# Forgetting attention in a two-layer trunk: negated scores, mask in the bias row, query blocks from last to first, normalisation moved from the probabilities to the output

## The chip, the cores and the metric

One core of a Trainium2 chip runs the whole kernel. The metric is the device time of one execution in microseconds (us); lower is better. A core has TensorE (PE in the profile, with its weight loads as PEld), VectorE (DVE), ScalarE (ACT), GpSimd (POOL), SyncE (SP, which issues the DMAs here), a working memory SBUF of 128 partitions and an accumulation memory PSUM of eight banks.

## The reference, cut to what matters

The trunk has two layers: attention and an MLP, then a state-space mixer and an MLP, each between RMS norms. Batch 1, 1024 positions, 1024 channels, 16 heads of 64. Only the attention is touched:

```python
proj = h @ w_in                     # q, k, v, gate (1024 columns each), f_logit (16)
q = rmsnorm(heads(q), q_gain)
k = rmsnorm(heads(k), k_gain)
log_f = log_sigmoid(f_logit + b_f)
c = cumsum(log_f, axis=1).transpose(0, 2, 1)
scale = HEAD_DIM ** -0.5
for blk in range(seq_len // Q_BLOCK):              # 8 blocks of 128 queries
    ...
    s = einsum('bhqd,bhkd->bhqk', qb, kb) * scale  # keys up to the block's end
    s = s + c[:, :, q0:k_end, None] - c[:, :, None, :k_end]
    s = where(mask, s, -inf)                       # causal
    p = softmax(s, axis=-1)
    outs.append(einsum('bhqk,bhkd->bhqd', p, vb))
o = concatenate(outs) ...
o = o * sigmoid(gate)
return o @ w_out
```

The term c of the query is the same along a row, so softmax drops it: the kernel adds only the key's term.

## The kernel before, in words

The kernel is written with a tile framework: the program names tiles, and the order of each engine's queue and all its waits are fixed when the kernel is built, from the order of writing, from priorities (`high_priority`), and from estimated durations. On the chip each engine then works its queue strictly in order. `weave` alternates between streams of work in the order of writing: each stream is a generator that yields a cost after each piece, and the stream that is least far through its total goes next.

The attention handles one pair of heads at a time (`fox`, line 613). Beside the attention of pair hp run the projections of pair hp+1 (`qkv`, 466) and the gate of pair hp-1 (`gate`, 506); beside the last pair only the gate before and the output weights. Products of fp32 data are made of parts rounded to fp32r: projections by `fm` (277) and `mm3` (271, lines 273 to 275) with three matmuls for high and low halves.

`forget_sum` (388) makes the running sum of the forget terms, with the sign turned so that it is minus c, and stores it to DRAM as `negc`. `attend` (525) goes through 128 units, 16 heads by 8 query blocks, block 0 first; block qb has (qb+1)x128 keys. For a unit:

- `load_bias` (531) brings the head's row of `negc` to all 128 partitions, as tile `An` (two buffers, SyncE's queue).
- `scores` (535) multiplies queries and keys into a PSUM slot of two banks (lines 543, 544; two such slots). VectorE adds the causal mask to the diagonal block (546), adds the bias row and takes the row maximum in one instruction (548, with a small accumulator read), and turns its sign (550). ScalarE takes the exponential with that as bias and accumulates the row sum (553). VectorE takes the reciprocal (554), and GpSimd multiplies the whole row block by it (555).
- `transposes` (557), one unit later, turns the probabilities by blocks of 128 on TensorE (567), four blocks to a PSUM bank. There is one bank for this (`PTB`). ScalarE copies the high part out (570, tile `pth`), VectorE the rest (571, `ptl`). These have three buffers each.
- `values` (573), after every second unit, multiplies with v (586) into one PSUM bank; after two such, ScalarE and VectorE add the halves into `o` (590, 591).

`qk_proj`, `qk_norm` and `v_proj` (400 to 464) leave their PSUM banks through ScalarE and VectorE (409 and 457 among them); line 437 copies the queries to the other half of the partitions on GpSimd. `gate` multiplies `o` by the sigmoid (518) and stores the result; the last pair's stays on the chip (`ogk`) and is split for the output product (254, 255). Weights come on SyncE's queue (232).

Of the kernel before, what the change touches and what calls it, by code (L numbers as in the profile page):

```python
# [11 lines left out]
AF = mybir.ActivationFunctionType  # L12
ALU = mybir.AluOpType

P = 128
D = 1024
NT = 8
NH = 16
HD = 64
FF = 2816  # L20
NF = FF // P
EPS = 1e-6
NEG = -1e30
NPG = 38
LNEXP = 'natural_log_exp_and_others'
MAGIC = 1.5 * 2.0 ** 23
# [6 lines left out]
PTB = (2,)  # L33
# [3 lines left out]
def f32(ap):  # L37
    return ap.bitcast(F32)
# [121 lines left out]
class Trunk:  # L160
# [178 lines left out]
    def fox_setup(self):  # L339
        nc, A, c = self.nc, self.A, self.cst  # L340
        self.bones = c.tile([P, P], F32R, name="bones")
        nc.vector.memset(f32(self.bones), 0.0)
        for i in range(2):
            nc.vector.memset(f32(self.bones[i * 64:i * 64 + 64, i * 64:i * 64 + 64]), 1.0)
        self.cmask = c.tile([P, P], F32, name="cmask")
        nc.gpsimd.memset(self.cmask, 0.0)
        nc.gpsimd.affine_select(out=self.cmask, in_=self.cmask, compare_op=ALU.is_ge, fill=NEG, base=0,
                                pattern=[[-1, P]], channel_multiplier=1)
        self.gcol = []
        for nm_, s in (("fox_q_gain", HD ** -0.5), ("fox_k_gain", 1.0)):  # L350
            t = c.tile([P, 1], F32, name=nm_ + "c")
            v = A[nm_]
            for i in range(2):
                nc.sync.dma_start(t[i * 64:i * 64 + 64, :],
                                  bass.AP(tensor=v.tensor, offset=v.offset, ap=[[1, HD], [1, 1]]))
            nc.vector.tensor_scalar_mul(t, t, -0.5 * s)
            self.gcol.append(t)
        self.bf = c.tile([NH, 1], F32, name="bf")
        v = A["fox_b_f"]
        nc.sync.dma_start(self.bf, bass.AP(tensor=v.tensor, offset=v.offset, ap=[[1, NH], [1, 1]]))  # L360
        self.wf = self.R("wf", (P, 8, 48), F32R)
        raw = self.R("wr", (P, 8, NH))
        nc.sync.dma_start(raw, A["fox_w_in"][0][:, 4 * D:4 * D + NH].rearrange("(k p) n -> p k n", p=P))
        nc.gpsimd.memset(f32(self.wf[:, :, NH:32]), 0.0)
        nc.gpsimd.tensor_copy(self.wf[:, :, 0:NH], raw)
        nc.gpsimd.tensor_sub(self.wf[:, :, 32:48], raw, f32(self.wf[:, :, 0:NH]))
        self.negc = self.dram("negc", [NH, D])

    def forget_logits(self, hT):
        nc, R = self.nc, self.R  # L370
# [17 lines left out]
    def forget_sum(self):  # L388

        nc = self.nc  # L390
        z, t1, ones = self.fgt
        nc.scalar.activation(t1, z, AF.Abs)
        nc.scalar.activation(t1, t1, AF.Exp, scale=-1.0)
        nc.scalar.activation(t1, t1, AF.Ln, bias=self.one[0:NH])
        nc.vector.tensor_scalar_mul(z, z, -1.0)
        nc.vector.scalar_tensor_tensor(t1, z, 0.0, t1, op0=ALU.max, op1=ALU.add)
        nc.vector.tensor_tensor_scan(z, ones, t1, 0.0, op0=ALU.mult, op1=ALU.add)
        nc.sync.dma_start(self.negc, z)

    def qk_proj(self, w, hT, hf, st):  # L400
        nc = self.nc
# [122 lines left out]

    def attend(self, c, o):

        nc = self.nc
        units = [(h, qb) for h in range(NH) for qb in range(8)]
        An, pt, Pt, pv = {}, {}, {}, {}

        def load_bias(h):
            An[h] = self.R("An")
            nc.sync.dma_start(An[h], self.bcast(self.negc[h:h + 1, :], D))

        def scores(h, qb):
            qh, ql = c[h // 2]["q"][h % 2 * 2:h % 2 * 2 + 2]
            k = c[h // 2]["k"][h % 2]
            nk = (qb + 1) * P
            qs = slice(qb * P, nk)
            ps = self.S("S")  # L540
            for c0 in range(0, nk, 512):
                c1 = min(c0 + 512, nk)
                nc.tensor.matmul(ps[:, c0:c1], qh[:, qs], k[:, c0:c1], start=True, stop=False)
                nc.tensor.matmul(ps[:, c0:c1], ql[:, qs], k[:, c0:c1], start=False, stop=True)
            with self.tc.high_priority(AHEAD):
                nc.vector.tensor_add(ps[:, qs], ps[:, qs], self.cmask)
                m, nm = self.small("mx"), self.small("nm")
                nc.vector.tensor_tensor_reduce(out=ps[:, :nk], in0=ps[:, :nk], in1=An[h][:, :nk], op0=ALU.add, op1=ALU.max,
                                               scale=1.0, scalar=-3e38, accum_out=m)
                nc.vector.tensor_scalar_mul(nm, m, -1.0)  # L550
            p = Pt[h, qb] = self.R("Pt")
            rs, ri = self.small("rs"), self.small("ri")
            nc.scalar.activation(p[:, :nk], ps[:, :nk], AF.Exp, bias=nm, accum_out=rs)
            nc.vector.reciprocal(ri, rs)  # L554
            nc.gpsimd.tensor_scalar(p[:, :nk], p[:, :nk], ri, 1.0, op0=ALU.mult, op1=ALU.mult)  # L555

        def transposes(h, qb):
            j, qq = qb // 2, qb % 2
            if qq == 0:
                ng = (2 * j + 2 + 3) // 4  # L560
                pt[h, j] = [(self.R("pth", (P, 4, 256), F32R), self.R("ptl", (P, 4, 256), F32R)) for _ in range(ng)]
            p = Pt.pop((h, qb))
            for g in range(0, qb + 1, 4):
                n = min(4, qb + 1 - g)
                p2 = self.pb(PTB, (P, 4, P))
                for i in range(n):
                    nc.tensor.transpose(p2[:, i], p[:, (g + i) * P:(g + i + 1) * P], self.ident)  # L567
                th, tl = pt[h, j][g // 4]
                dh, dl = th[:, 0:n, qq * P:qq * P + P], tl[:, 0:n, qq * P:qq * P + P]
                nc.scalar.copy(dh, p2[:, 0:n])  # L570
                nc.vector.tensor_sub(dl, p2[:, 0:n], f32(dh))  # L571

        def values(h, j):
            h2, vt = h % 2, c[h // 2]["v"]
            if h2 == 0 and j == 0:
                o[h // 2] = self.R("o")
            r = slice(h2 * 64, h2 * 64 + 64)
            if j % 2 == 0:
                pv[h] = self.pb(PVB)
            out = pv[h][:, (j % 2) * 256:(j % 2) * 256 + 256]  # L580
            last = 2 * j + 1
            t = pt.pop((h, j))
            seq = [(0, 0)] + [(kb, i) for kb in range(1, last + 1) for i in (0, 1)] + [(0, 1)]
            for n, (kb, i) in enumerate(seq):
                lo = P if kb == last else 0
                nc.tensor.matmul(out[:, lo:], vt[kb // 4][:, kb % 4, h2, :], t[kb // 4][i][:, kb % 4, lo:],
                                 start=(n == 0), stop=(n == len(seq) - 1))
            if j % 2:
                d = o[h // 2][r, (j // 2) * 512:(j // 2) * 512 + 512]
                nc.scalar.copy(d, pv[h][64 - h2 * 64:128 - h2 * 64])  # L590
                nc.vector.tensor_add(d, d, pv[h][r])

        load_bias(0)
        for i in range(len(units) + 3):
            hp = min(i, len(units) - 1) // 16
            if i < len(units):
                h, qb = units[i]
                if qb == 0:
                    yield 0.0, hp
                scores(h, qb)  # L600
                if qb == 5 and h + 1 < NH:
                    load_bias(h + 1)
                yield 0.16 * (qb + 1), hp
            if 1 <= i <= len(units):
                h, qb = units[i - 1]
                transposes(h, qb)
                yield 0.11 * (qb + 1), hp
            if i >= 3 and (i - 3) % 2 == 1:
                h, qb = units[i - 3]
                values(h, qb // 2)  # L610
                yield 0.22 * (qb + 1), hp
# [837 lines left out]
def trunk(ctx: ExitStack, tc: tile.TileContext, A, out):  # L1449
    T = Trunk(ctx, tc, A, out)  # L1450
    nc, R = T.nc, T.R
    rg = lambda a, b: list(range(a, b))
# [35 lines left out]
    for f in range(8):  # L1488
        T.plan(T.cols(A["s5_w_glu"][0], f * P)[:3] + (("glu",) * 2 if f == 0 else (None,) * 2))
        if f >= 1:  # L1490
# [11 lines left out]
          cc=[33], cp=[34, 13, 17], T=[33, 7, 14], M=[30, 16, 18], rot=[29, 10, 15], u=[25, 8, 9], Z=[4], k=[6],  # L1502
          S5=[26, 11, 3], Y=[27], W=[28, 32], gt=[31, 32], sg5=[33], gtk=[34])

    R.set(**{f"p{i}": [i] for i in [*range(7, 15), 35]}, vt=rg(15, 19), pth=rg(19, 22), ptl=rg(22, 25), pt=rg(25, 29) + [23, 24], An=[29, 30], Pt=[31, 32],
          o=[33, 34], x=[15, 16, 17, 18, 22, 13], y=[30, 12, 14], gn=[33], wf=[34], wr=[32], fg=[19, 20, 21])
    x0 = A["x"][0]
    hT = T.new_hT()
# [121 lines left out]
```

## Time and profile before

| | before |
|---|---|
| time, median of 3 runs | 2474.95 us (2472.84 to 2478.91) |
| the profiled execution's own time | 2474.52 us |
| its span in the profile | 2472.7 us |
| attention's period, one pair of heads | 79 us |
| mean granted TensorE clock | 0.99 |

The profile is of one execution. A row of groups reads: line, engine, operation, output and inputs with shapes, count, busy us and mean ns of one, idle time of the engine before them and what ended it. In a view of waits, "PEld ps L567 <- DVE ptl L571: 2.0, 5, 0.6" says that weight loads of line 567 waited 2.0 us in all, 5 times, at most 0.6 us, for VectorE's line 571. A matmul's end is modelled in the profile, so a busy TensorE is not one at its peak. In a timeline the columns are start, duration (us), engine, line, operation, and in brackets the idle time before with what ended it.

### The profile page before, as it was taken

What the parts mean: (1) busy time and instruction counts of PE and PEld (TensorE: products, weight loads), DVE (VectorE), ACT (ScalarE), POOL (GpSimd) and SP (SyncE); (2) the same over time, 40 slices, a digit from 0 to 9 for tenths busy, and PEclk for the clock granted to TensorE, in tenths of its full rate; (3) what the DMA queues carried; (4) which work ended last, traced back from release to release, by engine and by line L of the source; (5) the groups of instructions that cost most, each with busy time, mean ns of one, the idle gap of its engine ahead of it and who ended that gap; (6) DMA issues with size and microseconds to landing.
All of it is one profiled execution on the core that took longest, in us unless ns stands there. A gap on an engine that the chain in (4) does not pass through costs nothing.

```text
span 2472.7 us, 31528 instructions
## 1 busy us (share of the span) xinstructions
PE 2370.7 (96%) x11484; PEld 1938.5 (78%) x11484; DVE 1758.2 (71%) x3050; ACT 1177.2 (48%) x1989; POOL 554.0 (22%) x452
## 2 busy tenths in 40 slices
PE   7999999999998999999989989899999999999998
PEld 5777778777777778888877768788878888888886
DVE  6877877778778957666588785774686556555867
ACT  5766676667745343444434543332463333333434
POOL 3323222223200034545571241430000000000003
PEclk9999999999999999999999999999999999999999
DMA  4121111111243434343678742544334233337874
GB/s 128 54 60 43 43 44 52 44 43 56 87 148 97 122 116 130 118 133 113 225 248 273 268 158 74 153 144 127 108 100 130 90 115 103 98 111 248 287 237 160
DMA packets 251083, 314.50 MB, mean 127 GB/s; under 512 B 33888, under 2 KB 179488, under 8 KB 250928
## 3 DMA queue, kind: packets, MB, share of 16 engines
q1 hardware_dynamic: 250928, 312.50, 39.5%
q8 instruction: 90, 1.47, 0.2%
q14 instruction: 65, 0.53, 0.1%
HBM read 234.79 MB, written 77.66 MB: 126 GB/s over the span
## 4 chain that ended last, share of the span: by engine, by line
PE 53%; DVE 6%; DMA 2%; ACT 2%; issue 2%; POOL 1%; SPq 0%; DVEq 0%; ACTq 0%; POOLq 0%
PE ps L790 30%; PE ps L886 11%; PE ps L273 3%; PE ps L275 3%; PE ps L274 3%; DMA raw<-in_ffn_w_down_dram 1%; DVE wdl L255 1%; DMA raw<-in_s_w_in_dram 1%; DVE gl L255 1%; PE ps L1274 0%; POOL S L1256 0%; PE ps L1273 0%; PE ps L1232 0%; DVE y L315 0%; DMA gr<-g_d 0%
## 5 line engine op out<-in xcount | busy, mean ns | idle before, releaser
L790 PE MATMUL ps<-B,ah 128*128 128x512 f32 x1056 | 330.0, 394 | 4.0 <-ACT cc L1107 2.3
L886 PE MATMUL ps<-wdl,gh 128*128 128x512 f32 x616 | 243.8, 396 | 14.5 <-DVE wdl L255 13.7
L886 PE MATMUL ps<-wdh,gh 128*128 128x512 f32 x616 | 243.2, 395 | 6.5 <-DVE m L906 3.7
L886 PE MATMUL ps<-wdh,gl 128*128 128x512 f32 x616 | 242.7, 394 | 1.8 <-DVE gl L255 1.8
L790 PEld LDWEIGHTS ps<-B,ah 128*128 128x128 f32 x1056 | 200.7, 190 | 47.8 <-ACT cc L1107 2.7
L790 PE MATMUL ps<-ops,ah 128*128 128x512 f32 x704 | 218.1, 391 | 1.9 <-ACT s L830 1.9
L273 PE MATMUL ps<-hT,wh 128*128 128x512 f32 x512 | 207.8, 406 | 9.0 <-DVE pt L409 4.3
L555 POOL TENSOR_SCALAR Pt<-Pt,ri 128x128 f32<-128x128 f32 (+7 forms) x128 | 117.8, 921 | 415.5 <-DVE ri L554 327.0
L790 PE MATMUL ps<-B,al 128*128 128x512 f32 x528 | 207.4, 393 | 0.0
L274 PE MATMUL ps<-hT,wh 128*128 128x512 f32 x512 | 203.7, 398 | 0.0
L275 PE MATMUL ps<-hT,wl 128*128 128x512 f32 x512 | 203.0, 397 | 0.0
L1581 POOL TENSOR_TENSOR y<-m,s 128x512 f32<-128x512 f32 x4 | 7.2, 1794 | 765.7 <-DMA raw<-in_ffn_w_down_dram 756.8
L254 ACT CAST gh<-gr 128x1024 fp32r<-128x1024 f32 (+1 forms) x78 | 81.2, 1041 | 202.3 <-PE ps L886 138.3
L255 DVE TENSOR_TENSOR gl<-gr,gh 128x1024 fp32r<-128x1024 f32 (+1 forms) x78 | 110.3, 1416 | 82.1 <-ACT gh L254 79.0
L761 DVE TENSOR_TENSOR al<-raw,ah 128x1024 fp32r<-128x1024 f32 x88 | 112.9, 1283 | 64.1 <-ACT ah L760 64.0
L790 PEld LDWEIGHTS ps<-ops,ah 128*128 128x128 f32 x704 | 131.4, 188 | 30.9 <-ACT s L830 2.4
L886 PEld LDWEIGHTS ps<-wdl,gh 128*128 128x128 f32 x616 | 117.4, 191 | 42.9 <-DVE wdl L255 18.5
L760 ACT CAST ah<-raw 128x1024 fp32r<-128x1024 f32 x88 | 92.6, 1052 | 112.0 <-PE ps L790 107.2
L571 DVE TENSOR_TENSOR ptl<-ps,pth 128x512 fp32r<-128x512 f32 (+1 forms) x192 | 106.3, 554 | 55.2 <-ACT pth L570 50.0
L886 PEld LDWEIGHTS ps<-wdh,gh 128*128 128x128 f32 x616 | 117.6, 191 | 33.7 <-DVE m L906 4.1
L886 PEld LDWEIGHTS ps<-wdh,gl 128*128 128x128 f32 x616 | 117.5, 191 | 26.6 <-DVE gl L255 2.3
L570 ACT CAST pth<-ps 128x512 fp32r<-128x512 f32 (+1 forms) x192 | 91.8, 478 | 95.8 <-PE ps L567 83.7
(342 smaller groups left out, 5962.2 us busy)
## 6 DMA issues: line engine op xcount, KB each, us to landing
raw<-in_ffn_w_down_dram SPq DMA_DIRECT2D x98, 512.0 KB, 5.0
gr<-g_d SPq DMA_DIRECT2D x76, 512.0 KB, 4.5
raw<-in_ffn_w_gate_dram SPq DMA_DIRECT2D x44, 512.0 KB, 4.1
raw<-in_ffn_w_up_dram SPq DMA_DIRECT2D x44, 512.0 KB, 4.3
g_d<-s SPq DMA_DIRECT2D x66, 256.0 KB, 2.1
raw<-in_fox_w_in_dram SPq DMA_DIRECT2D x32, 512.0 KB, 4.1
g_d<-up SPq DMA_DIRECT2D x22, 512.0 KB, 2.7
g_d<-up SPq DMA_DIRECT2D x44, 256.0 KB, 2.7
```

Source lines behind the costliest of these rows:

```text
L254: self.nc.scalar.copy(h, src)
L255: self.lsub.tensor_sub(l, src, f32(h))
L273: mm(ps, lh, rh, start=start, stop=False)
L274: mm(ps, lh, rl, start=False, stop=False)
L275: mm(ps, ll, rh, start=False, stop=stop)
L555: nc.gpsimd.tensor_scalar(p[:, :nk], p[:, :nk], ri, 1.0, op0=ALU.mult, op1=ALU.mult)
L570: nc.scalar.copy(dh, p2[:, 0:n])
L571: nc.vector.tensor_sub(dl, p2[:, 0:n], f32(dh))
L760: nc.scalar.copy(h, src)
L761: V.tensor_sub(l, src, f32(h))
L790: nc.tensor.matmul(bank, x[:, k], y, start=start and k == i == 0, stop=True, skip_group_check=True)
L886: nc.tensor.matmul(bank, x[:, j, t], y[:, j], start=start and i == 0, stop=True, skip_group_check=True)
```

## The change

Scores are made negative: the query gain gets a minus sign, the stored sum is c itself, and what was a maximum becomes a minimum, which the exponential takes as its bias directly with scale -1. The mask is positive (1e30) and is added by GpSimd to the head's bias row, at the diagonal block's columns, ahead of each unit; since the blocks of a head now go from last to first, a masked block of the row is needed by no later unit. The probabilities stay undivided. The row sums of a pair's 16 units are gathered in one tile, transposed, inverted, stored to DRAM and read back as two broadcasts (64 partitions for each head), and GpSimd multiplies the pair's output `o` with them ahead of the gate. The order of `transposes` and `values` follows the reversed blocks, and the second group of transposes of a unit is written after one more yield. The tile of broadcast reciprocals has two buffers.

```diff
-NEG = -1e30
+FAR = 1e30
...
-        nc.gpsimd.affine_select(out=self.cmask, in_=self.cmask, compare_op=ALU.is_ge, fill=NEG, base=0,
+        nc.gpsimd.affine_select(out=self.cmask, in_=self.cmask, compare_op=ALU.is_ge, fill=FAR, base=0,
...
-        for nm_, s in (("fox_q_gain", HD ** -0.5), ("fox_k_gain", 1.0)):
+        for nm_, s in (("fox_q_gain", -HD ** -0.5), ("fox_k_gain", 1.0)):
...
-        self.negc = self.dram("negc", [NH, D])
+        self.csum = self.dram("csum", [NH, D])
+        self.ri_d = [self.dram(f"ri{hp}_d", [NH, P]) for hp in range(8)]
...
-        nc.vector.tensor_scalar_mul(z, z, -1.0)
-        nc.vector.scalar_tensor_tensor(t1, z, 0.0, t1, op0=ALU.max, op1=ALU.add)
+        nc.vector.scalar_tensor_tensor(t1, z, 0.0, t1, op0=ALU.min, op1=ALU.subtract)
         nc.vector.tensor_tensor_scan(z, ones, t1, 0.0, op0=ALU.mult, op1=ALU.add)
-        nc.sync.dma_start(self.negc, z)
+        nc.sync.dma_start(self.csum, z)
...
-        units = [(h, qb) for h in range(NH) for qb in range(8)]
-        An, pt, Pt, pv = {}, {}, {}, {}
+        units = [(h, qb) for h in range(NH) for qb in reversed(range(8))]
+        An, pt, Pt, pv, rs, ri = {}, {}, {}, {}, {}, {}
...
+            nc.gpsimd.tensor_add(An[h][:, qs], An[h][:, qs], self.cmask)
             ps = self.S("S")
...
             with self.tc.high_priority(AHEAD):
-                nc.vector.tensor_add(ps[:, qs], ps[:, qs], self.cmask)
-                m, nm = self.small("mx"), self.small("nm")
-                nc.vector.tensor_tensor_reduce(out=ps[:, :nk], in0=ps[:, :nk], in1=An[h][:, :nk], op0=ALU.add, op1=ALU.max,
-                                               scale=1.0, scalar=-3e38, accum_out=m)
-                nc.vector.tensor_scalar_mul(nm, m, -1.0)
+                m = self.small("mx")
+                nc.vector.tensor_tensor_reduce(out=ps[:, :nk], in0=ps[:, :nk], in1=An[h][:, :nk], op0=ALU.add, op1=ALU.min,
+                                               scale=1.0, scalar=3e38, accum_out=m)
             p = Pt[h, qb] = self.R("Pt")
-            rs, ri = self.small("rs"), self.small("ri")
-            nc.scalar.activation(p[:, :nk], ps[:, :nk], AF.Exp, bias=nm, accum_out=rs)
-            nc.vector.reciprocal(ri, rs)
-            nc.gpsimd.tensor_scalar(p[:, :nk], p[:, :nk], ri, 1.0, op0=ALU.mult, op1=ALU.mult)
+            if h // 2 not in rs:
+                rs[h // 2] = self.small("rs", (P, 2, 8))
+            nc.scalar.activation(p[:, :nk], ps[:, :nk], AF.Exp, bias=m, scale=-1.0,
+                                 accum_out=rs[h // 2][:, h % 2, qb:qb + 1])
+
+        def sums(hp):
+
+            p2, r, x = self.pb(PTB, (P, P))[0:16], self.small("ri", (16, P)), self.R("RI")
+            nc.tensor.transpose(p2, rs.pop(hp).rearrange("p a b -> p (a b)"), self.ident)
+            nc.vector.reciprocal(r, p2)
+            nc.sync.dma_start(self.ri_d[hp], r)
+            for i in range(2):
+                nc.sync.dma_start(x[i * 64:i * 64 + 64], self.bcast(self.ri_d[hp][i * 8:i * 8 + 8], D, 64))
+            ri[hp] = x
...
-            if qq == 0:
+            if qq:
...
             for g in range(0, qb + 1, 4):
                 n = min(4, qb + 1 - g)
+                if g:
+                    yield 0.11 * 4
...
-            if h2 == 0 and j == 0:
+            if h2 == 0 and j == 3:
                 o[h // 2] = self.R("o")
...
-            if j % 2 == 0:
+            if j % 2:
                 pv[h] = self.pb(PVB)
...
-            if j % 2:
+            if j % 2 == 0:
                 d = o[h // 2][r, (j // 2) * 512:(j // 2) * 512 + 512]
...
+                if h2 and j == 0:
+                    nc.gpsimd.tensor_mul(o[h // 2], o[h // 2], ri.pop(h // 2))
...
-                if qb == 0:
+                if qb == 7:
                     yield 0.0, hp
                 scores(h, qb)
-                if qb == 5 and h + 1 < NH:
+                if qb == 2 and h + 1 < NH:
                     load_bias(h + 1)
...
-                transposes(h, qb)
-                yield 0.11 * (qb + 1), hp
+                for x in transposes(h, qb):
+                    yield x, hp
+                yield 0.11 * (qb % 4 + 1), hp
+                if h % 2 and qb == 0:
+                    sums(h // 2)
```

More of the change, by code (lines that the diff above doesn't have):

```diff
@@ L527, in attend @@
         nc = self.nc
-        units = [(h, qb) for h in range(NH) for qb in range(8)]
-        An, pt, Pt, pv = {}, {}, {}, {}
+        units = [(h, qb) for h in range(NH) for qb in reversed(range(8))]
+        An, pt, Pt, pv, rs, ri = {}, {}, {}, {}, {}, {}
         def load_bias(h):
             An[h] = self.R("An")
-            nc.sync.dma_start(An[h], self.bcast(self.negc[h:h + 1, :], D))
+            nc.sync.dma_start(An[h], self.bcast(self.csum[h:h + 1, :], D))
         def scores(h, qb):
@@ L1503, in trunk @@
           S5=[26, 11, 3], Y=[27], W=[28, 32], gt=[31, 32], sg5=[33], gtk=[34])
-    R.set(**{f"p{i}": [i] for i in [*range(7, 15), 35]}, vt=rg(15, 19), pth=rg(19, 22), ptl=rg(22, 25), pt=rg(25, 29) + [23, 24], An=[29, 30], Pt=[31, 32],
+    R.set(**{f"p{i}": [i] for i in [*range(7, 15), 35]}, vt=rg(15, 19), pth=rg(19, 22), ptl=rg(22, 25), pt=rg(25, 29) + [23, 24], An=[29, 30], Pt=[31, 32], RI=[36, 37],
           o=[33, 34], x=[15, 16, 17, 18, 22, 13], y=[30, 12, 14], gn=[33], wf=[34], wr=[32], fg=[19, 20, 21])
```

## The prediction

> **What bounds the kernel now.** I read the page first, then the windows cut to the period of the attention, then who waited for whom inside one such period, then the groups by line, and at last the timeline of a few units and of the end of the attention.
>
> ```profile
> span 2472.7 us, 31528 instructions
> ...
> PE 2370.7 (96%) x11484; PEld 1938.5 (78%) x11484; DVE 1758.2 (71%) x3050; ACT 1177.2 (48%) x1989; POOL 554.0 (22%) x452
> ```
>
> TensorE looks full: 96% busy. Only the attention is touched, so I looked for its own period. A head pair (16 units of one head and one block of queries, beside the projections of the next pair and the gate of the pair before) comes round every 79 us with the same instruction counts, and the last pair is thinner:
>
> ```profile
> core 0: us, PE busy (x) PEld busy (x) DVE busy (x) ACT busy (x) POOL busy (x), PEclk, DMA share, GB/s
> 220.00:299.00 79.00, 76.32 (x408) 62.19 (x408) 60.51 (x144) 53.84 (x103) 21.14 (x24) 1.00 0.17 48
> 299.00:378.00 79.00, 76.27 (x408) 62.18 (x408) 60.51 (x144) 53.84 (x103) 21.13 (x24) 1.00 0.16 47
> ...
> 615.00:690.00 75.00, 72.47 (x396) 57.45 (x395) 53.26 (x125) 48.30 (x90) 15.37 (x17) 1.00 0.33 104
> ```
>
> TensorE is the only engine near its limit: 76.3 of 79 us, VectorE 60.5 (77%), at a full clock. So the whole change can win at most TensorE's waiting, whatever work it takes off VectorE and GpSimd. By the matmul row that is 79 - 76.3 = 2.7 us a pair. The weight loads, which start each matmul, show more, because a matmul's modelled end covers part of the pause behind it:
>
> ```profile
> engine line waited for: us in total, times, longest us
> PEld ps L567 <- DVE ptl L571: 2.0, 5, 0.6
> PEld ps L567 <- POOL Pt L555: 1.6, 3, 0.7
> PEld ps L273 <- DVE pt L409: 1.3, 2, 1.1
> PEld ps L567 <- issue: 0.7, 3, 0.3
> PEld ps L543 <- ACT Pt L553: 0.6, 1, 0.6
> PEld ps L273 <- ACT pt L457: 0.5, 1, 0.5
> PEld ps L273 <- DVE vt L452: 0.4, 1, 0.4
> PEld ps L586 <- ACT pth L570: 0.3, 1, 0.3
> ```
>
> The sum is 7.4 us. The matmul rows of the same window give the lower price of two of these:
>
> ```profile
> PE ps L273 <- DVE pt L409: 0.9, 1, 0.9
> PE ps L567 <- POOL Pt L555: 0.3, 1, 0.3
> PE ps L567 <- DVE ptl L571: 0.3, 1, 0.3
> ```
>
> [...] I use both as ends.
>
> **The change part by part.** What it takes away stands in four groups:
>
> ```profile
> L555 POOL TENSOR_SCALAR Pt<-Pt,ri 128x128 f32<-128x128 f32 (+7 forms) x128 | 117.8, 921 | 415.5 <-DVE ri L554 327.0 <-DVE nm L550 47.4 <-PE ps L586 17.5
> ...
> L546 DVE TENSOR_TENSOR ps<-ps,cmask 128x128 f32<-128x128 f32 x128 | 37.4, 297 | 24.3 <-PE ps L544 23.6
> ...
> L554 DVE RECIPROCAL ri<-rs 128x1 f32<-128x1 f32 x128 | 20.3, 159 | 15.1 <-ACT Pt L553 13.2
> ...
> L550 DVE TENSOR_SCALAR nm<-mx 128x1 f32<-128x1 f32 x128 | 18.8, 147 | 0.4
> ```
>
> VectorE loses 37.4 + 20.3 + 18.8 = 76.5 us, 9.6 a pair, and goes from 60.5 to about 51 of 79 us (77% to 64%). None of this is TensorE time; it counts only through waits. GpSimd loses 117.8 us. The chain of one unit, from scores to transposes, loses the mask (297 ns), the negation (147), the reciprocal (159) and the GpSimd scaling (921): 1.5 us before any hand-over between engines. The exponential and the reduction with its accumulator read stay, with the same sizes; I cost min for max and the scale of -1 at nothing.
>
> What it adds. First, 128 GpSimd additions of the mask to the bias row, 128x128 with two inputs in SBUF. No row has just this; the nearest are:
>
> ```profile
> L312 POOL TENSOR_TENSOR y<-x,gn 128x1024 f32<-128x1024 f32 x4 | 9.5, 2369 | 6.3 <-ACT y L296 6.3
> L1144 POOL TENSOR_TENSOR R<-R,ident 16x128 f32<-16x128 f32 x8 | 8.8, 1101 | 102.1 <-DVE S L773 102.1
> ...
> L555 POOL TENSOR_SCALAR Pt<-Pt,ri 128x128 f32<-128x128 f32 x16 | 6.8, 423 | 18.3 <-DVE ri L554 13.6 <-PE ps L567 4.7
> ...
> L1156 POOL TENSOR_TENSOR s5w<-s5w,R 16x128 f32<-16x128 f32 x8 | 4.6, 579 | 0.0
> ```
>
> So 0.42 to 1.1 us; I take 0.5, between the one-input and the shorter two-input row. 128 of them are 64 us: less than GpSimd gives up. But the addition stands between two reductions: block qb's columns of the bias may be written only after the reduction of block qb+1 has read them, and must be written before block qb's own. How long that keeps VectorE is seen from two hand-overs of before:
>
> ```profile
> 227.50 0.43 DVE L548 CUSTOM_DVE_ANT_0 ps<-ps,An 128x256 f32<-128x256 f32 x1
> ...
> 228.35 0.56 DVE L548 CUSTOM_DVE_ANT_0 ps<-ps,An 128x384 f32<-128x384 f32 x1
> ...
> 228.94 0.16 DVE L554 RECIPROCAL ri<-rs 128x1 f32<-128x1 f32 x1
> ...
> 229.27 0.48 POOL L555 TENSOR_SCALAR Pt<-Pt,ri 128x256 f32<-128x256 f32 x1 [6.55 <-DVE nm L550]
> ```
>
> The reciprocal ends at 229.10 and GpSimd starts at 229.27: 0.17 us a hand-over. Two of them and 0.5 are 0.84 us. These two reductions start 0.85 us apart, 0.42 from the end of one to the start of the next, so the addition would hold the second back by about 0.4 us; but a pair's 16 units are spread over 79 us, 4.9 each, and most have room. The wait sits on VectorE's queue, and behind it lie the subtractions of L571 and the evacuation of L409, on which TensorE waits. The bound is nothing to 0.84 us for each of 112 units (the first block of a head waits only for its bias): 0 to 94 us of VectorE (it can't gain: nothing is taken away by it), of which the part that reaches TensorE I put at 0.1 us a pair.
>
> [...]
>
> Second, once a pair: a transpose of the 16 columns of sums (TensorE; the 128-column transposes below take 279 ns, pipelined; 16 columns are no more, and I take 0.2 us), a reciprocal, one store, two broadcast loads and a 128x1024 GpSimd product on the output.
>
> ```profile
> L567 PE MATMUL ps<-ident,Pt 128*128 128x128 f32 x576 | 98.1, 279 | 10.0 <-DVE ptl L571 4.5 <-POOL Pt L555 2.3 <-DVE nm L550 0.7
> ```
>
> The product is L312's 2.4 us, and mask additions queue behind it; the pair's last output is ready only after three units of the next pair, some 15 us at 4.9 each. The round trip of the sums is, from the store of the forget sums and the loads of the bias,
>
> ```profile
> DMA to landing us min/median/max: 1.9/1.9/1.9
> ...
> DMA to landing us min/median/max: 3.4/4.6/7.7
> ```
>
> 1.9 + 4.6 = 6.5 us, with the issues about 8: ready first. On SyncE's queue the weight loads stand behind the store's wait for the reciprocal; those run a buffer or two ahead, so I cost it at nothing; without that lead it is up to those 8 us a pair.
>
> Third, the order. Units shrink within a head instead of growing, and the first one needs both halves of the projections; gate matmuls (24 a half) stand there to cover. The second group of transposes is now written behind some other work, so the wait for the one transpose bank (ptl, 2.0 us) gets cover.
>
> Sum for a pair, loads' price first, matmuls' price second: GpSimd's wait 1.6 falls to 0.3 (the exponential is next late): -1.3, or -0.3; ptl halves: -1.0, or -0.15; L409 and L452, VectorE being a sixth less loaded, lose a third: -0.6, or -0.3; the scores' wait for the exponential: -0.2, or 0. Together -3.1, or -0.75; I take -2.0, near the middle since some of each pause is covered. Added: 0.2 + 0.1. Net -1.7, and 8 pairs give -13.6 us.
>
> The end of the attention:
>
> ```profile
> 670.74 1.12 ACT L553 ACTIVATE Pt<-ps,nm 128x1024 f32<-128x1024 f32 x1
> ...
> 685.06 2.17 DVE L518 TENSOR_TENSOR ogk<-o,pt 128x1024 f32<-128x1024 f32 x1
> ```
>
> From the last exponential to the gated output are 16.5 us. After the change the last unit is the small one, but the chain has the round trip (8), the product (2.4), the gate (2.2) and some 1.5 of exponential, transpose and hand-overs: 14, or 17 with the longest landing. I take no difference; the bounds are 3 us either way, and the first output product's matmuls cover it now.
>
> Against the profiled execution's own 2474.52 us (its span 2472.7), 0.4 under the median of 2474.95, this is 2461.
>
> **The rivals.** (a) The mask addition becomes the wait: each reduction, and what queues behind it, stands for GpSimd. For it: two reductions come 0.42 us apart above, and GpSimd's copies of the queries (L437) share its queue. Against: 4.9 us a unit. It makes the kernel slower by over 7.4 us from the point where 13.6 + 7.4 = 21 us reach TensorE, 0.19 us on each of 112 units. If half the units lose 0.84 and half of that reaches TensorE, 24 us are lost and the time is 2485. (b) The waits return at the next late step: the transposes wait for the exponential, TensorE's queue being laid out anew around the shorter chain. Only the matmul rows' 0.75 less 0.3 is won, 4 us: 2471, within 0.3%. (c) The whole of the loads' pauses on VectorE, GpSimd and the exponential goes: 2.0 + 1.6 + 1.3 + 0.6 + 0.4 = 5.9, less the 0.3 and about a quarter that was covered anyway: 4.1 a pair, 33 us, 2442. (d) The change doesn't shorten the chain at all, because the sums' round trip comes after the output is ready and the product holds the additions: 2.4 us a pair, 19 us over eight, takes back more than the gain: 2480, still within 0.3%.
>
> **How the numbers follow.** 0.3% (7.4 us) is about what a measurement can tell here. Forecast 0.47 (its own range 2452 to 2467), (c) 0.15, (b) 0.18, (a) 0.15, (d) 0.05. Faster: 0.47 + 0.15 and little from (b), 0.62; same: (b) and part of (d), 0.21; slower 0.17. The range runs from (c) at 2440 to short of (a), 2482.
>
> **What would show it.** Right: a pair's period near 77.3 us; VectorE at about 51 us a pair; no wait of L567 on GpSimd, under 1.2 us on ptl; the mask addition near 0.5 us and no more than 0.4 us of VectorE's pauses on it a unit. Wrong: TensorE waiting for the exponential as long as for GpSimd before (b); VectorE idle on the addition, and L571 late behind it (a); a period of 75 (c); GpSimd idle on the loads of the reciprocals (d).

## The result and the profile after

| | before | after |
|---|---|---|
| median of 7 runs each, us | 2474.95 (2472.84 to 2479.55) | 2484.30 (2480.76 to 2485.92) |
| ratio to before, 95% interval | | 1.0026 (1.0017 to 1.0035) |
| span of the profiled execution, us | 2472.7 | 2483.1 |

The ratio and its interval are the estimate on record over these runs; the quotient of the two medians is 1.0038. The kernel is slower, by a quarter to four tenths of a per cent, and the forecast of 2461 us was on the wrong side.

The page of the changed kernel, its first part:

```profile
span 2483.1 us, 31134 instructions
...
PE 2375.1 (96%) x11492; PEld 1938.0 (78%) x11492; DVE 1723.3 (69%) x2673; ACT 1180.4 (48%) x1989; POOL 531.3 (21%) x460
```

VectorE and GpSimd have lost work, and the span has grown by 10.4 us. The page alone does not say where. Landmarks of the two traces do (us from the start of each span):

| | before | after | after less before |
|---|---|---|---|
| first reduction of the second pair | 139.8 | 141.9 | +2.1 |
| first reduction of the last pair | 614.0 | 609.9 | -4.1 |
| last exponential starts | 670.7 | 667.8 | -2.9 |
| last gated output (`ogk`) ready | 687.2 | 690.3 | +3.1 |
| last matmul of the attention's output product starts | 766.7 | 773.0 | +6.3 |
| first matmul of the MLP | 772.0 | 779.1 | +7.1 |
| span | 2472.7 | 2483.1 | +10.4 |

(A pair's first reduction is that of block 0 before and of block 7 after.) In its middle the changed kernel wins: the period of a pair is 78.0 us, where it was 79.0. It is 2.9 us ahead at the last exponential and 3.1 us behind at the gated output that follows from it. So the loss lies at the end of the attention and in the product after it. The last 3.3 us come after the first MLP matmul, in code that the change doesn't touch. There the clock record of the trace has 55.4 us at half speed, against 48.7 before; 6.7 us more at half speed can cost about 3.4, an estimate: half of them. What brought them there I did not trace.

The windows of the changed kernel, one steady pair and the last pair (columns: stretch, length, busy us of PE, PEld, DVE, ACT, POOL, granted clock, DMA):

```profile
297.40:375.40 78.00, 75.79 (x412) 61.60 (x410) 55.72 (x96) 54.06 (x102) 18.38 (x25) 1.00 0.19 55
...
609.80:692.00 82.20, 74.96 (x396) 58.41 (x397) 47.65 (x81) 45.51 (x86) 12.68 (x17) 0.99 0.37 112
```

VectorE fell from 60.5 to 55.7 us a pair, not to the 51 that the removed instructions come to: in the kernel before, the durations of VectorE's groups in one pair add up to 69.9 us against 60.5 busy, since short instructions overlap their neighbours (one reduction runs from 227.50 to 227.93 us, and its accumulator read starts at 227.85), and so a sum of durations overstates what goes. The waits of the weight loads in that steady pair:

```profile
engine line waited for: us in total, times, longest us
PEld ps L582 <- DVE ptl L586: 4.0, 12, 0.7
PEld ps L273 <- DVE pt L410: 2.1, 2, 1.6
PEld ps L582 <- ACT Pt L557: 0.5, 1, 0.5
PEld ps L451 <- ACT pt L458: 0.4, 1, 0.4
PEld ps L273 <- DVE vt L453: 0.3, 1, 0.3
```

The wait for GpSimd (1.6 us) is gone and 0.5 for the exponential stands in its place; that for the scores' bank (0.6) is gone too. But the wait for the single transpose bank has doubled from 2.0 to 4.0, and that for L410 (L409 before), the copy of the projections out of their bank, has grown from 1.3 to 2.1. The matmul rows of the same window price these two quite differently; of the bank's 4.0 us only 0.3 stands there, as before:

```profile
PE ps L273 <- DVE pt L410: 1.2, 1, 1.2
PE ps L582 <- DVE ptl L586: 0.3, 1, 0.3
```

And the end, in the timeline of the changed kernel:

```profile
667.81 0.37 ACT L557 ACTIVATE Pt<-ps,mx 128x128 f32<-128x128 f32 x1
...
671.80 0.33 PE L582 MATMUL ps<-ident,Pt 128*128 128x128 f32 x1
...
672.37 0.94 ACT L254 CAST wh<-raw 128x896 fp32r<-128x896 f32 x1 [1.95 <-DMA raw<-og_d]
...
673.22 0.26 ACT L585 CAST pth<-ps 128x128 fp32r<-128x128 f32 x1
...
673.35 1.09 DVE L255 TENSOR_TENSOR wl<-raw,wh 128x896 fp32r<-128x896 f32 x1 [1.61 <-ACT wh L254]
...
674.36 0.28 DVE L586 TENSOR_TENSOR ptl<-ps,pth 128x128 fp32r<-128x128 f32 x1
...
674.70 0.09 PEld L563 LDWEIGHTS ps<-ident,rs 128*16 128x16 f32 x1 [0.53 <-DVE ptl L586]
...
675.01 0.94 DVE L564 RECIPROCAL ri<-ps 16x128 f32<-16x128 f32 x1 [0.37 <-PE ps L563]
...
675.99 0.65 SPq L565 DMA_DIRECT2D ri_d<-ri  x1
...
680.43 1.09 SPq L567 DMA_DIRECT2D RI<-ri_d  x2
...
685.90 2.34 POOL L608 TENSOR_TENSOR o<-o,RI 128x1024 f32<-128x1024 f32 x1 [25.12 <-DMA RI<-ri_d]
...
688.28 1.99 DVE L519 TENSOR_TENSOR ogk<-o,pt 128x1024 f32<-128x1024 f32 x1 [10.34 <-POOL o L608]
...
690.30 0.50 ACT L254 CAST wh<-ogk 128x128 fp32r<-128x128 f32 x2 [14.59 <-DVE ogk L519]
...
690.66 0.79 PE L273 MATMUL ps<-woh,wh 128*128 128x512 f32 x1 [5.30 <-ACT wh L254]
```

From the last exponential to the gated output it is 22.5 us. The transpose of the sums stands 6.9 us behind the exponential, since it is written behind the last unit's own transposes and needs the same bank. The bank itself is held by what stands in two other queues: the last transposes are done at 672.13, but ScalarE's copy out of the bank (L585) stands behind a split of the earlier pairs' gated outputs (L254), which waits 1.95 us for their load, and so starts only at 673.22; VectorE's (L586) stands behind the other half of that split (L255, 1.09 us). So the bank comes free only at 674.64. GpSimd has stood idle for 25 us when the reciprocals arrive; VectorE waits 10.3 us for GpSimd, and TensorE 5.3 us for the split of the gated output. Before, that pause was 0.74:

```profile
687.61 0.50 PE L273 MATMUL ps<-woh,wh 128*128 128x512 f32 x1 [0.74 <-ACT wh L254]
```

TensorE had done everything else: seven eighths of the first two output products, which both need the last pair only for their last eighth. Behind these two eighths it pauses once more, for the norm of the first product, 4.0 us against 0.7 before:

```profile
699.05 0.76 PE L273 MATMUL ps<-woh,wh 128*128 128x512 f32 x1 [4.04 <-DVE y L315]
```

Then the clock (columns as above):

```profile
684.00:690.60 6.60, 1.36 (x6) 0.78 (x5) 1.99 (x1) 0.29 (x2) 2.34 (x1) 0.97 0.06 14
690.60:716.00 25.40, 21.31 (x85) 17.09 (x86) 16.28 (x35) 13.99 (x29) 0.00 (x0) 0.81 0.36 118
690.15:693.56 3.41, 2.90 (x7) 2.33 (x8) 0.62 (x3) 0.86 (x3) 0.00 (x0) 0.50 0.00 0
696.98:703.80 6.82, 4.75 (x11) 3.80 (x12) 4.79 (x12) 3.51 (x8) 0.00 (x0) 0.50 0.57 187
```

In the 25.4 us behind the first pause the granted clock is 0.81 and 85 matmuls are done; in the same stretch of the kernel before it was 1.00, with 117:

```profile
690.60:716.00 25.40, 24.71 (x117) 20.05 (x116) 20.14 (x43) 15.15 (x30) 0.00 (x0) 1.00 0.50 166
```

The first matmul behind the pause lasts 0.79 us (the row at 690.66), its counterpart before 0.50 (687.61). In the two stretches at half speed TensorE is busy for 2.90 + 4.75 = 7.65 us; matmuls of 512 columns start 0.43 us apart there (691.25, 691.67, 692.10), and 0.23 apart before at full speed (687.95, 688.18, 688.41). At full speed that work would take about half as long, so the slow clock costs about 3.8 us, an estimate from these rows. From the last exponential to the last matmul of the output product 9.2 us are lost (2.9 ahead to 6.3 behind), so the clock is not the larger part.

### The profile page after: what moved, and what is told of

It is laid out like the page before. It is cut to its first block, busy times and chain, and to the rows that moved or that the text cites. A ratio compares the mean times of both kernels' runs of the same rounds, so it can differ in the third digit from the quotient of the medians.

```text
span 2483.1 us, 31134 instructions
## 1 busy us (share of the span) xinstructions
PE 2375.1 (96%) x11492; PEld 1938.0 (78%) x11492; DVE 1723.3 (69%) x2673; ACT 1180.4 (48%) x1989; POOL 531.3 (21%) x460
## 4 chain that ended last, share of the span: by engine, by line
PE 68%; DVE 15%; ACT 7%; issue 4%; DMA 4%; POOL 1%; SPq 0%; DVEq 0%; ACTq 0%; POOLq 0%
PE ps L810 31%; PE ps L906 10%; PE ps L273 6%; PE ps L274 6%; PE ps L275 6%; PE ps L582 2%; PE ps L601 2%; DVE ps L552 2%; ACT Pt L557 1%; DVE p L435 1%; ACT wh L254 1%; DMA raw<-in_ffn_w_down_dram 1%; DVE wdl L255 1%; DMA raw<-in_s_w_in_dram 1%; DVE ptl L586 1%
## 5 line engine op out<-in xcount | busy, mean ns | idle before, releaser
L273 PE MATMUL ps<-hT,wh 128*128 128x512 f32 x512 | 209.1, 409 | 9.2 <-DVE pt L410 7.3
L254 ACT CAST gh<-gr 128x1024 fp32r<-128x1024 f32 (+1 forms) x78 | 81.2, 1041 | 202.1 <-PE ps L906 120.5
L255 DVE TENSOR_TENSOR gl<-gr,gh 128x1024 fp32r<-128x1024 f32 (+1 forms) x78 | 110.7, 1422 | 79.8 <-ACT gh L254 77.3
L586 DVE TENSOR_TENSOR ptl<-ps,pth 128x512 fp32r<-128x512 f32 x192 | 106.6, 555 | 85.7 <-ACT pth L585 81.0
L544 POOL TENSOR_TENSOR An<-An,cmask 128x128 f32<-128x128 f32 x128 | 75.6, 592 | 398.8 <-DVE mx L552 373.6
L781 DVE TENSOR_TENSOR al<-raw,ah 128x1024 fp32r<-128x1024 f32 x88 | 118.5, 1349 | 52.1 <-ACT ah L780 51.8
L810 PE MATMUL ps<-ops,al 128*128 128x512 f32 x352 | 137.0, 389 | 0.0
```

The costliest lines, as they stand in the source:

```text
L254: self.nc.scalar.copy(h, src)
L255: self.lsub.tensor_sub(l, src, f32(h))
L273: mm(ps, lh, rh, start=start, stop=False)
L544: nc.gpsimd.tensor_add(An[h][:, qs], An[h][:, qs], self.cmask)
L781: V.tensor_sub(l, src, f32(h))
L810: nc.tensor.matmul(bank, x[:, k], y, start=start and k == i == 0, stop=True, skip_group_check=True)
```

## The experiments

Each ran against the kernel before on the same chip, where that kernel's median was 2477.0 to 2477.2 us; ratios are to before, with 95% intervals. The pair period is read in each trace from one pair's first reduction to the next pair's, in the steady middle. Eleven kernels in three groups.

**The end of the attention.** My theory after the result: the chain of the end decides, and the slow clock adds to it. The rivals: the pairs themselves, or the clock alone.

**1. The last pair divided on the probabilities.** In `scores`, and `sums` and the product on `o` skipped for pair 7:

```diff
+            if h // 2 == 7:
+                r1, i1 = self.small("r1"), self.small("i1")
+                nc.scalar.activation(p[:, :nk], ps[:, :nk], AF.Exp, bias=m, scale=-1.0, accum_out=r1)
+                nc.vector.reciprocal(i1, r1)
+                nc.gpsimd.tensor_scalar(p[:, :nk], p[:, :nk], i1, 1.0, op0=ALU.mult, op1=ALU.mult)
+                return
```

> The changed kernel, but in the last pair of heads the probabilities are divided by their sums as before (reciprocal on VectorE, product on GpSimd, 16 units); no sums, round trip or product on the output for that pair. Theory (the end of the attention): the chain from the last exponential over the sums' round trip to the gated output (22.5 us from 667.8 to 690.3) ends after TensorE has run dry, and the pause slows its clock; without the round trip the pause of 5.3 us is gone, the one of 4.0 us falls to below 1, no half-speed window falls between 700 and 716 us, and the 1 us a pair that the middle gained shows: 2484.3 - 4.6 - 3.3 - 3 = about 2473, between 2469 and 2476, not slower than before. Rival (the loss lies in the pairs themselves, in the doubled wait for the transpose bank): the end hardly matters, 2481 or more.

Measured: 2469.94 us, ratio 0.9975 (0.9967 to 0.9983); pair period 78.0. The gated output in its timeline:

```profile
668.48 0.37 ACT L557 ACTIVATE Pt<-ps,mx 128x128 f32<-128x128 f32 x1
...
678.21 2.15 DVE L519 TENSOR_TENSOR ogk<-o,pt 128x1024 f32<-128x1024 f32 x1
...
680.74 0.50 PE L273 MATMUL ps<-woh,wh 128*128 128x512 f32 x1 [0.74 <-ACT wh L254]
```

The chain is 11.9 us (668.48 to 680.36) in place of 22.5, the pause 0.74 in place of 5.30. Its windows show no slow clock behind it:

```profile
690.60:716.00 25.40, 25.07 (x122) 20.32 (x122) 18.78 (x39) 13.39 (x29) 0.00 (x0) 1.00 0.46 151
```

Only the division of one pair in eight differs from the changed kernel, and the kernel goes from slower to faster than before. The round trip in the last pair costs 0.5% by the ratios (1.0026 against 0.9975), about 12.6 us. The theory holds; the pairs are not the loss.

**2. TensorE kept busy through the pause.** In `out_proj`, with the last eighths of the two products ordered behind it:

```diff
+            last = nc.tensor.matmul(d, sl[:, 6, :], ws[6][0][:, 0:512], start=True, stop=True)
+            for _ in range(22):
+                with self.tc.issue_after(last.ins):
+                    last = nc.tensor.matmul(d, sl[:, 6, :], ws[6][0][:, 0:512], start=True, stop=True)
```

> The changed kernel with 23 extra matmuls of 512 columns into a spare bank (their result is not used) behind the first seven eighths of the first two output products, so that TensorE works through the 5.3 us pause. The gated output still comes at about 690.3 us. Rival (the clock alone: the pause would cost nothing if it did not slow the clock): two half-speed windows of together 10.2 us are gone and with them nearly the whole loss, 2476 or less. Theory (the chain itself is late, the clock adds to it): the half-speed windows behind the pause go, worth at most 5 us, about 2 to 4 since a second pause stays; the time is 2480 to 2483.

Measured: 2479.79 us, ratio 1.0014 (1.0005 to 1.0022). Against the change's own 1.0026 that is 0.0012, some 3 us, though the intervals overlap. Its window:

```profile
690.60:716.00 25.40, 20.16 (x82) 15.62 (x81) 16.66 (x33) 12.39 (x25) 0.45 (x1) 0.87 0.30 99
```

The clock rises from 0.81 to 0.87 only. The experiment filled its pause only in part: its gated output comes at 693.1 us, 2.8 later than in the change, so TensorE still pauses 1.8 us in front of the last eighths, and 3.3 us for the norm of the first product behind them; with each pause come 3.4 us at half speed. So it does not separate the two rivals by itself. That the clock is not the whole cause rests on the 3.8 us worked out above; these 3 us (6.5 by the medians) fit it, but don't settle it.

**5. The sums sent ahead of the last transposes.** In `attend`:

```diff
+                if i == len(units):
+                    sums(7)
                 for x in transposes(h, qb):
                     yield x, hp
                 yield 0.11 * (qb % 4 + 1), hp
-                if h % 2 and qb == 0:
+                if h % 2 and qb == 0 and i < len(units):
```

> The changed kernel with one move: in the last pair the sums are transposed, inverted and sent on their round trip ahead of the last unit's own transposes, not behind them. Theory (the chain of the end decides): the sums' transpose started 6.4 us after the last exponential; now it starts within 1 to 2 us of it, so the gated output comes about 4 to 5 us earlier (685 to 686 us), the pause in front of the last matmuls shrinks from 5.3 to under 2 us and the clock is not lowered behind it: 2484.3 less 4 to 8, that is 2476 to 2480, level with before. Rival (only removing the division helps): no change, 2483 or more.

Measured: 2479.81 us, ratio 1.0007 (0.9999 to 1.0016), level with before as the theory had it. The place was only half reached:

```profile
671.92 0.09 PEld L563 LDWEIGHTS ps<-ident,rs 128*16 128x16 f32 x1 [0.26 <-DVE ptl L586]
...
685.37 1.99 DVE L519 TENSOR_TENSOR ogk<-o,pt 128x1024 f32<-128x1024 f32 x1 [7.88 <-POOL o L608]
...
687.75 0.50 PE L273 MATMUL ps<-woh,wh 128*128 128x512 f32 x1 [2.23 <-ACT wh L254]
```

The sums' transpose still stands 4.0 us behind the start of the exponential (6.9 in the change; I had expected 1 to 2), because the bank holds the unit before. The output comes 2.9 us earlier and the pause falls from 5.3 to 2.2 us. The clock, which I expected to stay up, still falls behind it (0.87 over 690.6 to 716). Moving one step of the chain earlier, without removing any work, gave back some three quarters of the loss.

**The parts in the steady pair.** Order and division are two halves of the change, and each can stand alone.

**3. Order, sign and mask, without the division.** Every unit divides as in experiment 1's edit; no sums, no product on `o`.

> Negated scores, reversed blocks and the mask in the bias row as in the change, but the probabilities divided by their sums in every unit as before (GpSimd product), no sums tile, round trip or product on the output. Theory: without the round trip the end is short (small last unit), so this is no slower than before: 2468 to 2476; the pair period is 78 to 79 us. Rival (the reversed order or the mask on GpSimd is what costs): 2480 or more.

Measured: 2493.60 us, ratio 1.0071 (1.0059 to 1.0083); pair period 81.0. My theory fell here: the end was indeed short (`ogk` 10 us behind the last exponential), but each pair was 2.0 us longer than before. In its steady pair TensorE waits in front of the transposes, for the bank (`ptl`) and for their input (`Pt`):

```profile
PE ps L582 <- DVE ptl L586: 2.3, 4, 1.0
PE ps L582 <- POOL Pt L558: 1.5, 2, 1.1
PE ps L273 <- DVE pt L410: 0.8, 1, 0.8
```

**4. The division alone.** The kernel before, with the change's `sums` and product:

```diff
-            nc.vector.reciprocal(ri, rs)
-            nc.gpsimd.tensor_scalar(p[:, :nk], p[:, :nk], ri, 1.0, op0=ALU.mult, op1=ALU.mult)
...
+                if h2 and j == 3:
+                    nc.gpsimd.tensor_mul(o[h // 2], o[h // 2], ri.pop(h // 2))
...
+                if h % 2 and qb == 7:
+                    sums(h // 2)
```

> The kernel before (blocks first to last, mask and maximum on VectorE, positive scores) with only the division moved: sums gathered, transposed, inverted, stored and read back, product on the output on GpSimd. Theory: the round trip now starts after a full-size last unit, so the gated output comes later than in the changed kernel (about 693 us or more) and the time is 2484 to 2492. Rival (the loss needs the reversed order): 2470 to 2478.

Measured: 2483.71 us, ratio 1.0027 (1.0016 to 1.0038); pair period 77.2; gated output at 693.6 us, though the last exponential starts at 664.5. So the division alone wins 1.8 us a pair, more than the whole change does, and loses more than all of it at the end, as the theory said (the time is 0.3 us below its range).

**6. The division alone, last pair divided early.** Experiment 4 with the edit of experiment 1.

> The kernel before with the division moved to the output in the first seven pairs (period 77.2 us in the run with the division alone, 79.0 before), and the last pair divided on the probabilities as before. Theory: it keeps 1.8 us on each of six periods and loses nothing at the end: 11 us less than before, about 2464 where before is 2475, a ratio of 0.994 to 0.997. Rival (the gain of the middle is given back elsewhere): a ratio of 0.998 or more.

Measured: 2471.78 us, ratio 0.9980 (0.9970 to 0.9989); pair period 77.2. It wins, but half of what I expected, and the rival, that something is given back, is right by that half. It starts its last pair at 604.2 us, 9.8 ahead of before, and has its gated output at 682.2, only 5.0 ahead. In the last pair TensorE pauses anew:

```profile
PE ps L602 <- ACT pth L586: 2.1, 2, 1.8
PE ps L583 <- DVE nm L551: 1.9, 1, 1.9
PE ps L273 <- ACT Pt L555: 1.4, 1, 1.4
```

The clock falls with these pauses, which it does not in experiment 9's last pair (second row):

```profile
660.00:690.00 30.00, 28.86 (x134) 23.20 (x135) 16.50 (x25) 15.07 (x25) 2.13 (x2) 0.90 0.46 147
660.00:690.00 30.00, 28.92 (x142) 22.54 (x141) 17.14 (x31) 14.08 (x26) 1.12 (x1) 1.00 0.51 159
```

A tenth of 30 us is up to 3 of the 4.8 us that the last pair gives back. There each unit goes back to the long chain, beside less projection work; why just these three waits come late I did not test.

**9. The same with negated scores.** The query gain's sign, the minimum and the exponential's scale as in the change; no instruction for the sign; forward blocks, mask on VectorE.

> As the division alone with the last pair divided early, plus negated scores (minimum as the exponential's bias, scale -1, so no sign turn on VectorE): blocks first to last, mask on VectorE in PSUM. 128 VectorE instructions of 147 ns less, 2.4 us a pair of VectorE. Theory (VectorE's load reaches TensorE only through a few waits): the period falls by 0 to 0.4 us a pair, the time by 0 to 3 us against the run without the negation. Rival (VectorE's latency in the chain of a unit is what TensorE waits for): 0.5 us a pair or more, 4 us or more.

Measured: 2468.62 us, ratio 0.9961 (0.9949 to 0.9974); pair period 76.95. The period fell by 0.25 us, within the theory's range. The time fell more than the range said (0.9980 to 0.9961, 4.7 us, with intervals that overlap); its last pair is also shorter, 76.3 us from the first reduction to the gated output against 78.0 in experiment 6, at a full clock.

**7. Reversed blocks with the mask on VectorE.** Experiment 1 with one line moved:

```diff
-            nc.gpsimd.tensor_add(An[h][:, qs], An[h][:, qs], self.cmask)
...
+                nc.vector.tensor_add(ps[:, qs], ps[:, qs], self.cmask)
```

> Reversed blocks, negated scores, last pair divided early (as in the first experiment), but the mask added by VectorE to the scores in PSUM as in the kernel before, so no GpSimd addition between two reductions. The first experiment had a pair period of 78.0 us, forward blocks with the mask on VectorE 77.2. Theory A (the reversed order costs the 0.8 us): the period stays at 78 us or more, time about 2470. Theory B (the GpSimd addition costs it): the period falls to about 77.2, time about 2465.

Measured: 2494.60 us, ratio 1.0063 (1.0051 to 1.0076); pair period 81.8. Theory B fell; of theory A the sign holds, but the period is 3.8 us above its 78 and the time 25 us above its 2470. It differs from experiment 9 in the order of the blocks and the yield, and costs 4.8 us a pair more; and the mask on GpSimd, which theory B blamed, is worth 3.8 us a pair in this order. Its steady pair, TensorE's waits and the window:

```profile
PE ps L588 <- DVE ptl L592: 2.6, 3, 2.0
PE ps L451 <- ACT pt L458: 1.1, 1, 1.1
PE ps L273 <- DVE pt L410: 1.0, 2, 0.7
```

```profile
386.60:468.40 81.80, 76.91 (x412) 63.27 (x411) 59.11 (x113) 53.55 (x103) 8.96 (x9) 0.98 0.18 52
```

TensorE is idle for 4.9 us of this period, against 2.2 in experiment 1; the one wait of 2.0 us for the transpose bank is most of the difference. Behind it comes a stretch at half speed, once in every pair:

```profile
410.39:413.80 3.41, 3.41 (x11) 2.76 (x11) 1.96 (x3) 1.84 (x3) 0.00 (x0) 0.50 0.21 84
```

It costs about 1.7 us more, an estimate: half of 3.41, as the starts of the matmuls in the change show for half speed (0.43 us apart, 0.23 at full). Wait and clock together are 3.7 of the 3.8 us.

**11. The mask addition left out.** Experiment 1 without the GpSimd addition; the causal mask is not applied.

> Reversed blocks with the last pair divided early, with the GpSimd mask addition left out: the causal mask is not applied at all, so this times only the removal of that link between two reductions. Rival (a) of the prediction (the addition makes the reductions wait, and TensorE with them): the period falls from 78.0 to 77.4 us or less. If the addition is covered, as the 4.4 us of VectorE pauses on it in the whole changed kernel suggest: 77.7 to 78.3 us.

Measured: 2466.47 us, ratio 0.9955 (0.9942 to 0.9969); pair period 77.4 against 78.0. So the addition does cost 0.6 us a pair: just what I had put down as the sign of rival (a), and six times my 0.1, but far below the 21 us in all (2.6 a pair) that rival (a) needed to make the kernel slower by 7.4.

**8 and 10. The yield.** Experiment 1 without the yield, and experiment 9 with it:

```diff
-                if g:
-                    yield 0.11 * 4
```

> Reversed blocks, GpSimd mask, last pair divided early (the first experiment, period 78.0 us), without the added yield, so the second group of transposes of a unit is written right behind the first. If the yield gives the single transpose bank cover, as the prediction had it, the wait of the transposes for ptl (4.0 us a pair in the changed kernel) rises and the period goes to 78.5 us or more. If the builder's own order makes the yield idle, the period stays within 0.2 us of 78.0.

> Forward blocks, negated scores, mask on VectorE, division moved to the output except in the last pair (period 76.95 us, ratio 0.996 to before), plus the yield between the two groups of transposes. If the yield gives cover, the wait for ptl (4.1 us a pair) falls and the period goes below 76.7 us; if not, it stays within 0.3 us of 76.95.

Measured: 2470.03 us, ratio 0.9973 (0.9963 to 0.9984), period 78.05 without; 2467.88 us, ratio 0.9964 (0.9951 to 0.9978), period 76.95 with. The yield does next to nothing in either order; the wait for the bank stays at 4.1 to 4.3 us a pair.

The periods together, us a pair (all reversed rows have negated scores):

| blocks, mask | divided on the probabilities | divided in the output |
|---|---|---|
| forward, VectorE | 79.0 (before) | 77.2; 76.95 with negated scores |
| reversed, GpSimd | 81.0 | 78.0 (the change) |
| reversed, VectorE | | 81.8 |

## Why the prediction was wrong

**The bound was read rightly.** In the pairs VectorE and GpSimd lost work (4.8 and 2.8 us of busy time a pair) and the period fell by only 1.0 us, as it should if their work counts only where TensorE waits for it.

**The step that failed is the end of the attention:** "14, or 17 with the longest landing. I take no difference; [...] the first output product's matmuls cover it now." It measured 22.5. Term by term: exponential, transpose and hand-overs up to the end of the reciprocal were put at 1.5 us and took 8.1 (667.81 to 675.95), because I priced the operations and not the bank that the sums' transpose has to wait for, with the split and the load in front of the copies that free it, nor a reciprocal of 0.94 us. The round trip was put at 8 and took 9.9: the loads are issued only when the store has landed, at 680.43, 4.4 us after its issue, three times the median of the earlier pairs' stores (1.4 us). The product was 2.34 and the gate 1.99, as priced. The cover had no room either: TensorE reached the last eighth at 685.36, where before it was 686.87. The prediction's bounds for the whole end were 3 us either way; from 16.5 to 22.5 it grew by 6.0. Experiments 1 and 5 show this cause: shortened by 2.9 us, the chain gives back most of the loss; shortened by half, all of it, and the middle's gain appears.

**The clock was missing from the sum.** With each of the two pauses of 5.3 and 4.0 us came a stretch at half speed; together these cost some 3.8 us by the rows above, for which the sum had no term.

**The middle.** Forecast -1.7 us a pair, measured -1.0. Right: GpSimd's wait goes and the exponential is next late (0.3 forecast, 0.5 measured), and the scores' wait falls. Wrong: "the wait for the one transpose bank (ptl, 2.0 us) gets cover". By the weight loads it doubled, and experiments 8 and 10 show that the yield, which was to give the cover, does next to nothing. But that doubling cost little: by the matmul rows it is 0.3 as before, and experiments 9 and 10, the shortest complete periods, have 4.1 by the loads too. Wrong too: "Third, the order", to which I gave no price. With the mask on VectorE, reversed blocks cost 4.8 us a pair against forward ones; reversed blocks with the mask on GpSimd cost 1.05 against forward ones with it on VectorE (78.0 against 76.95). In that comparison the wait that differs by as much is L273's for the copy of the projections, which I had put down to lose a third: 1.2 us by the matmul rows in the change (0.9 before), and absent from the matmul rows of experiment 9's steady pair:

```profile
PE ps L581 <- DVE ptl L585: 0.8, 3, 0.4
PE ps L273 <- DVE vt L452: 0.2, 1, 0.2
```

That it is the cause is not shown; no run moved that copy alone. All queues are laid out anew with every edit, so one wait of 2 us can come or go, as in experiment 7. The sum also counted eight pairs; only the six periods between the second pair and the last show the gain, 6.2 us in all, and the second pair starts 2.1 us later than before.

**GpSimd's addition.** The price was right (0.5 taken, a median of 0.46 measured; the mean of 0.59 has some long ones in it). Its group in the changed kernel, and VectorE's wait for it:

```profile
L544 POOL TENSOR_TENSOR An<-An,cmask 128x128 f32<-128x128 f32 x128 | 75.6, 592 | 398.8 <-DVE mx L552 373.6 <-DMA An<-csum 24.9
```

```profile
DVE ps L552 <- POOL An L544: 4.4, 8, 0.6
```

VectorE waited for it 8 times in 128, 4.4 us in all, so rival (a) did not happen. The addition takes longer than VectorE's addition before, a median of 0.46 us (L544) against 0.29 (L546), more than half as long again, and that addition had one input in PSUM. Yet in this order the slower engine was the better place (a period of 78.0 us in experiment 1, 81.8 in experiment 7): the time of one instruction does not price the queue it leaves.

**The rivals.** None of the four was it. The 2485 of (a) is near the measured time by chance, since the wait it rests on did not come. Nearest as a mechanism was (d), a round trip that ends after the output is ready; but it was the last pair alone, at a place where I had seen the chain and called it covered. The result lies 2.3 us above the end of the range. Two slips change nothing: of the matmul rows' waits the prediction says two and shows three, and its range starts at 2440 where its own (c) is 2442.

## What to carry to other kernels

Here work moved from every step to the end of a block was hidden in the steady state and bare in the last block. So price the last block on its own, with every queue and bank that its chain passes, and keep the old form there if the new one is longer. When the middle gets faster, the cover at the end is over sooner too (1.5 us here). Experiments 9 and 10 are the best complete versions found (ratios 0.9961 and 0.9964): forward order, negated scores, division in the output, last pair divided early.

## What the runs showed of the hardware

In these traces some short pauses of TensorE come with a lower clock. With the pauses of 5.3 and 4.0 us in the changed kernel it was 0.81 of full clock over 25 us; in experiment 7 a pause of 2.0 us in each pair was followed by 3.4 us at half speed, 0.98 over the pair. Behind pauses of 0.7 us (before and experiment 1, at the same place) it stayed at 1.00 (690.6 to 716 us), and so it did in experiment 9's last pair, which has one of 1.6 us (604 to 690 us). The shortest of these pauses with a lower clock behind it is the one of 1.8 us in experiment 2, with 3.4 us at half speed. Whether the length of a pause alone decides, no run shows. A store of 8 KB to DRAM landed in 1.4 us in the middle of the attention (0.18 of the DMA engines' time in use there) and in 4.4 us at its end (0.88 in use from 676.0 to 680.4, by loads for what follows); that the load is the reason was not tested apart.
